# Add and GELU on one core: one load and one store with 64 KB rows in place of two each with 32 KB rows

## Chip, cores, metric

One core of one Trainium2 chip. The metric is device time in microseconds (us) of one execution. Executions of one kernel agree within some 0.3 to 0.5%.

## The reference

```
x, y: float32, 1024 x 4096
z = x + y
out = 0.5 * z * (1 + tanh(sqrt(2/pi) * (z + 0.044715 * z**3)))
```

The kernel uses the same function in the form z * sigmoid(c1 * (z + 0.044715 z^3)). It reads 33.55 MB and writes 16.78 MB.

## The kernel before

Each of the 128 partitions holds 8 rows of x in one piece: TOT = 32768 columns of float32, 128 KB. One tile z keeps all of it, first x, then x + y, then the result. y passes through two buffers of 8192 columns. I call 8192 columns a quarter. The compute engines work in 32 chunks of 1024 columns, while transfers have sizes of their own:

```python
YS = 8192
CH = 1024
PS = 4
loads = [2048, 6144, 8192, 8192, 8192]
stores = [8192, 8192, 8192, 4096, 4096]
...
def load_x(i):
    a, b = lr[i]
    nc.sync.dma_start(out=zt[:, a:b], in_=xv[:, a:b])
def load_y(i):                       # the same into yt[quarter]
    ...
def store(i):
    a, b = sr[i]
    nc.sync.dma_start(out=ov[:, a:b], in_=zt[:, a:b])
...
sp = []
for i in range(len(loads)):
    sp += [(load_x, i), (load_y, i)]
sp += [(store, i) for i in range(len(stores))]
```

All transfers are issued by SP (SyncE), in this order, into one queue. The other engines are POOL (GpSimd), DVE (VectorE) and ACT (ScalarE); PSUM is the second on-chip memory, beside the main one, SBUF. The engines' part per chunk: `add` (POOL; DVE for chunk 0), `sq` (ACT, into PSUM), `stt` (DVE), `sig` (ACT), `mul` (DVE, back into z). DVE runs `mul` of chunk c after `stt` of chunk c+1:

```python
for i in range(-3, C + 1):
    if 0 <= i < C:
        dve.append((stt, i))
        acts.append((sig, i))
    if 0 <= i - 1 < C:
        dve.append((mul, i - 1))
    ...
```

And a y load waits for the adds that free its buffer, a store for the multiplies of its columns.

## Time and profile before

| | before |
|---|---|
| median of 3 executions at the outset | 123.27 us (123.16 to 123.56) |
| span of the profiled execution | 121.5 us |
| busiest compute engine | DVE, 75.5 us (62%) |
| packets of the queue, share of 16 engines' span | 2160, 97.2% |

How to read it: a "span" runs from the first to the last instruction. The 16 DMA engines share a transfer's 128 partition rows, one row to a packet: 8 rows per engine and transfer, then one small packet that signals completion. A share near 100% for the queue means that all 16 engines are moving data nearly all the time. A line of a timeline reads: start in us, duration in us, engine (a q marks its sequencer, which issues transfers), line of the kernel, operation, output<-inputs, count, and in brackets the idle time before it and what ended it. The prediction below shows the lines of before.

### The profile page before, as it was taken

The numbers are of one execution on the slowest core, as the hardware profiler recorded it, in microseconds if no ns is written. First come the engines' busy times: TensorE is split into PE (matmuls) and PEld (weight loads), VectorE is DVE, ScalarE is ACT, GpSimd is POOL, SyncE is SP. The second block draws the span as 40 slices with busy tenths as digits, with TensorE's granted clock in tenths as the row PEclk, the third lists the DMA queues.
The fourth block names the chain that finished last, engine by engine and source line by source line (L and its number), as shares of the span: only waits on it lengthen the run. The fifth ranks groups of instructions, "written<-read, shape, count | busy, mean of one in ns | idle before, by whom it ended". The sixth has DMA issues, their size and how long they took to land.

```text
span 121.5 us, 248 instructions
## 1 busy us (share of the span) xinstructions
DVE 75.5 (62%) x66; ACT 63.8 (52%) x66; POOL 73.0 (60%) x35
## 2 busy tenths in 40 slices
DVE  0035700039999209999996999995999999500000
ACT  4004400068886028788767887883878878100000
POOL 0028000499990099999969999959999990000000
DMA  3999999998989999999999999899999999999993
GB/s 89 421 440 494 413 389 494 391 496 367 496 378 486 389 475 389 475 389 475 389 475 389 475 389 475 345 432 434 424 432 432 442 421 442 421 442 389 426 437 130
DMA packets 2162, 50.35 MB, mean 415 GB/s; under 512 B 240, under 2 KB 240, under 8 KB 240
## 3 DMA queue, kind: packets, MB, share of 16 engines
q1 hardware_dynamic: 2160, 50.33, 97.2%
q14 instruction: 2, 0.02, 0.0%
HBM read 33.55 MB, written 16.78 MB: 414 GB/s over the span
## 4 chain that ended last, share of the span: by engine, by line
DMA 49%; POOL 17%; DVE 16%; SPq 2%; ACT 1%; issue 0%; POOLq 0%
DMA y<-in_y_dram 49%; POOL z L87 17%; DVE z L107 8%; DVE w L98 8%; SPq L70 1%; SPq L77 1%; ACT w L92 1%; POOLq L87 0%
## 5 line engine op out<-in xcount | busy, mean ns | idle before, releaser
L87 POOL TENSOR_TENSOR z<-z,y 128x1024 f32<-128x1024 f32 x31 | 72.8, 2389 | 26.9 <-DMA y<-in_y_dram 26.9
L92 ACT ACTIVATE w<-z 128x1024 f32<-128x1024 f32 x32 | 32.9, 1028 | 38.7 <-POOL z L87 31.4
L98 DVE SCALAR_TENSOR_TENSOR w<-w,z 128x1024 f32<-128x1024 f32 x32 | 39.4, 1232 | 21.1 <-ACT w L92 21.1
L107 DVE TENSOR_TENSOR z<-w,z 128x1024 f32<-128x1024 f32 x32 | 38.8, 1214 | 0.0
L103 ACT ACTIVATE w<-w 128x1024 f32<-128x1024 f32 x32 | 31.4, 981 | 0.4 <-DVE w L98 0.4
L87 DVE TENSOR_TENSOR z<-z,y 128x1024 f32<-128x1024 f32 x1 | 1.2, 1224 | 7.3 <-DMA y<-in_y_dram 7.3
L146 ACT ACT_TABLE_LOAD x1 | 1.3, 1283 | 0.7 <-PEq L172 0.7
L145 DVE MEMSET one<- 128x1 f32 x1 | 0.1, 59 | 0.8 <-PEq L172 0.8
L172 POOL MEMSET const-float32-0.0<- 128x1 f32 x1 | 0.1, 98 | 0.2 <-issue 0.2
L146 ACT ACTIVATE one<-one 128x1 f32<-128x1 f32 x1 | 0.2, 203 | 0.0
L172 POOL MEMSET const-bfloat16-1.0<- 128x1 bf16 x1 | 0.1, 101 | 0.0
L172 POOL MEMSET const-uint8-127<- 128x1 uint8 x1 | 0.1, 101 | 0.0
L172 POOL MEMSET const-float32-1.0<- 128x1 f32 x1 | 0.1, 98 | 0.0
## 6 DMA issues: line engine op xcount, KB each, us to landing
z<-in_x_dram SPq DMA_DIRECT2D x3, 4096.0 KB, 34.2
y<-in_y_dram SPq DMA_DIRECT2D x3, 4096.0 KB, 24.8
out_dram<-z SPq DMA_DIRECT2D x3, 4096.0 KB, 30.3
out_dram<-z SPq DMA_DIRECT2D x2, 2048.0 KB, 17.4
z<-in_x_dram SPq DMA_DIRECT2D x1, 3072.0 KB, 13.8
y<-in_y_dram SPq DMA_DIRECT2D x1, 3072.0 KB, 20.6
z<-in_x_dram SPq DMA_DIRECT2D x1, 1024.0 KB, 4.9
y<-in_y_dram SPq DMA_DIRECT2D x1, 1024.0 KB, 6.9
```

The costliest lines, as they stand in the source:

```text
L70: nc.sync.dma_start(out=zt[:, a:b], in_=xv[:, a:b])
L77: nc.sync.dma_start(out=yt[s][:, o : o + b - a], in_=yv[:, a:b])
L87: eng.tensor_add(out=zt[:, a:b], in0=zt[:, a:b], in1=yt[s][:, o : o + b - a])
L92: nc.scalar.activation(out=wt[c], in_=zt[:, a:b], func=act.Square, scale=root)
L98: nc.vector.scalar_tensor_tensor(out=wt[c], in0=wt[c], scalar=c1, in1=zt[:, a:b], op0=alu.add, op1=alu.mult)
L103: nc.scalar.activation(out=wt[c], in_=wt[c], func=act.Sigmoid)
L107: nc.vector.tensor_mul(out=zt[:, a:b], in0=wt[c], in1=zt[:, a:b])
L145: nc.vector.memset(one, 0.0)
L146: nc.scalar.activation(out=one, in_=one, func=act.Sigmoid)
L172: nc = _bacc.Bacc("TRN2", target_bir_lowering=False, num_devices=1)
```

## The change

The intent is fewer, longer transfers. Two of the five x loads become one, ahead of y of the third quarter, and two of the five stores become one:

```diff
-    loads = [2048, 6144, 8192, 8192, 8192]
-    stores = [8192, 8192, 8192, 4096, 4096]
+    loads_x = [2048, 6144, 8192, 16384]
+    loads_y = [2048, 6144, 8192, 8192, 8192]
+    stores = [16384, 8192, 4096, 4096]
...
-    for i in range(len(loads)):
-        sp += [(load_x, i), (load_y, i)]
+    for i, (a, b) in enumerate(lr):
+        sp += [(load_x, k) for k, r in enumerate(xr) if r[0] == a] + [(load_y, i)]
...
-        add: lambda c: [(f, i) for i in over(lr, *cr[c]) for f in (load_x, load_y)],
+        add: lambda c: [(load_x, i) for i in over(xr, *cr[c])]
+        + [(load_y, i) for i in over(lr, *cr[c])],
```

(Cut: the helper that makes the ranges, and `load_x` reading its own list.)

More of the change, by code (lines that the diff above doesn't have):

```diff
@@ L50, in ranges @@
         return [(e - f, e) for e, f in zip(ends, sizes)]
-    lr, sr, cr = ranges(loads), ranges(stores), ranges([CH] * (TOT // CH))
+    xr, lr, sr = ranges(loads_x), ranges(loads_y), ranges(stores)
+    cr = ranges([CH] * (TOT // CH))
     C = len(cr)
@@ L68, in load_x @@
     def load_x(i):
-        a, b = lr[i]
+        a, b = xr[i]
         nc.sync.dma_start(out=zt[:, a:b], in_=xv[:, a:b])
```

## The prediction

> **What bounds the kernel now.** I read the page first: the engine shares, the DMA slices and the queue line.
>
> ```profile
> DVE 75.5 (62%) x66; ACT 63.8 (52%) x66; POOL 73.0 (60%) x35
> ...
> DMA  3999999998989999999999999899999999999993
> GB/s 89 421 440 494 413 389 494 391 496 367 496 378 486 389 475 389 475 389 475 389 475 389 475 389 475 345 432 434 424 432 432 442 421 442 421 442 389 426 437 130
> DMA packets 2162, 50.35 MB, mean 415 GB/s; under 512 B 240, under 2 KB 240, under 8 KB 240
> ...
> q1 hardware_dynamic: 2160, 50.33, 97.2%
> ```
>
> No compute engine passes 62%, while the packets of the one queue fill 97.2% of 16 engines' span: 0.972 x 121.5 = 118.1 us of DMA time. The DMA digits are 9 nearly everywhere between the first and last slices. The packet count has an exact reading: 15 transfers x (128 rows + 16 small ones) = 2160, so one row of one transfer is one packet, and each engine carries 8 rows and one small packet (the 240 under 512 B, which signal completion) per transfer.
>
> Second, busy shares by stretch, to see whether the queue ever runs dry (columns: stretch, length, busy time of DVE, ACT and POOL, clock, DMA share, GB/s):
>
> ```profile
> 1.70:11.70 10.00, 2.41 (x2) 1.58 (x4) 3.39 (x1) 1.00 1.01 406
> 11.70:60.60 48.90, 31.21 (x28) 27.17 (x28) 32.22 (x14) 1.00 1.00 432
> 60.60:77.60 17.00, 16.06 (x15) 13.60 (x14) 16.06 (x8) 1.00 1.00 432
> 77.60:81.20 3.60, 3.60 (x4) 2.88 (x3) 2.63 (x2) 1.00 1.16 428
> 81.20:120.20 39.00, 22.19 (x20) 17.57 (x19) 18.52 (x8) 1.00 0.97 418
> ```
>
> From 1.7 to 77.6 us the DMA share is 1.00: loads run head to tail. Packets are counted at their start, so 1.16 and 0.97 are neighbours to be read together. The packet records are finer. First packet 1.74 us, last 120.19 us, last completion seen 120.56 us. Transfers end, on their first engine, at 41.23 (y, second quarter), 50.94 (x, third), 60.65 (y, third), 70.36 (x, fourth), 80.62 (y, fourth), then the stores at 90.30, 99.98, 109.66, 114.52 and 119.38. A 4 MB transfer takes 9.7 us, except the last load, 10.26: its last two packets per engine, from 77.6 us on, take 1.3 to 1.8 us instead of 1.21. That loss of about 0.6 us, at the turn from loads to stores, is the only one inside the stream.
>
> Third, the chain of waits, then the last DMA issue in order of time.
>
> ```profile
> DMA 49%; POOL 17%; DVE 16%; SPq 2%; ACT 1%; issue 0%; POOLq 0%
> ```
>
> ```profile
> 104.84 0.33 SPq L81 DMA_DIRECT2D out_dram<-z  x1
> ```
>
> Read alone, the chain suggests that POOL and DVE matter. But it stops at the last multiply; the last store is issued at 104.84 us and waits behind 9.7 us of queued stores. Compute has that much slack at the end. The bound is the byte stream of the DMA queue.
>
> **What the Trainium skill says.** "DMA: Bandwidth & Descriptors", section "Where 436 GB/s comes from", gives a ceiling of 435 GB/s for the 16 ports. The trace agrees: 432 GB/s over 11.70 to 77.60 us. Larger transfers cannot go faster than that; only per-row cost can be saved.
>
> The same page, section "Why small descriptors are slow (HBM only)", speaks of a fixed overhead of about 3 cycles per packet. The packet records fit the kind: median 309, 611, 912 and 1213 ns for rows of 8, 16, 24 and 32 KB. Each 8 KB adds 301 to 302 ns, which leaves about 8 ns fixed per row. A small packet takes 9 ns.
>
> "SBUF — State Buffer", section "The DMA setup-cost knee", puts roughly 2 us on every transfer. Taken as a price per transfer it would promise 4 us here. This trace disagrees with using it so in a queue that is kept full: one transfer's 9 ns signal is followed at once by the next one's first row. The fixed cost shows only where the queue is empty: the first issue starts at 0.74 us and its first packet at 1.74, 1.0 us later.
>
> **The change, part by part.** The order of instructions on DVE, ACT and POOL is unchanged; SP issues two transfers fewer. x of quarters 3 and 4 becomes one transfer ahead of y of quarter 3; the stores of quarters 1 and 2 become one.
>
> Removed: each merge halves 8 rows per engine from two packets to one and drops one small packet: 8 x 8 + 9 = 73 ns. Two merges give 0.15 us. I estimate a 64 KB row at 2 x 1213 - 8 = 2418 ns. Two issues of about 0.4 us on SP go too, but they lie beside a full queue: 0.
>
> Moved: y of quarter 3 now follows all of x, one 4 MB transfer later. It ends where x of quarter 4 ended, less 0.07. The rest is worked from these two rows:
>
> ```profile
> 61.72 18.52 POOL L87 TENSOR_TENSOR z<-z,y 128x1024 f32<-128x1024 f32 x8 [0.94 <-DMA y<-in_y_dram]
> 81.67 18.52 POOL L87 TENSOR_TENSOR z<-z,y 128x1024 f32<-128x1024 f32 x8 [1.43 <-DMA y<-in_y_dram]
> ```
>
> - Adds of quarter 3 start at 61.72 + 9.71 - 0.07 = 71.36 instead of 61.72; POOL idles some 10 us before them.
> - Adds of quarter 4 find their y landed at 81.5, but POOL is busy to 71.36 + 18.52 = 89.88. They start there instead of at 81.67: all later compute is 8.21 us later, bound by POOL (16 adds x 2.315 in one run) rather than by arrivals.
>
> Each store must be issued 1.0 us before the queue reaches it (the delay of the first load):
> - First two quarters: DVE's order puts the multiply of chunk 15 behind chunk 16, so this store waits for quarter 3's first add. Before, the second store was issued 5.84 us after that add's start (67.56); now 71.36 + 5.84 = 77.20, first packet possible at 78.2. The loads end at 80.55. Slack 2.3 us.
> - Quarter 3: issued at 87.9 before (the last semaphore wait on the store line ends there), now 96.1, ready 97.1, due at 109.66 - 9.68 - 0.15 = 99.83. Slack 2.7 us.
> - First half of quarter 4: its last multiply ended near 96.7, now 104.9, ready 105.9, due 109.5. Slack 3.6 us.
> - Last half: 104.84 + 8.21 = 113.05, ready 114.05; due at 114.52 - 0.15 = 114.37 on the first engine and 115.17 on the slowest. Slack 0.3 us on the first engine, 1.1 us on the one that sets the end.
>
> So about 8.2 us of the tail slack goes, and none of it becomes a wait that ends later. Sum: 123.27 - 0.15 = 123.12, with a whisker for the last store: 123.1 us.
>
> **Rivals.** (a) The compute tail becomes the bound. If the queue restarts in 1.5 us rather than 1.0, or POOL runs a few per cent slower without its pause, the last store is late by 0.3 to 1 us: 123.4 to 124.1. For it: the 0.3 us is thin. Against it: the slow engine has 1.1 us. Also, "SBUF — State Buffer", section "Who interferes with whom", says GpSimd and DVE contend when a DVE instruction has two SBUF inputs; after the first chunk DVE always reads one operand from PSUM. The trace agrees: the one POOL add that ran beside DVE's own add took 3.39 us, the 16 above 18.52 / 8 = 2.315 us.
>
> (b) 64 KB rows are moved differently: cut into 32 KB pieces, saving only the two small packets (0.02 us: 123.25), or at a worse rate. A quarter of the bytes loaded plus half of those stored, 16.8 MB, use such rows, or 38.7 us of queue time; each 1% of rate costs 0.4 us. Against a bad rate: the four sizes lie on one straight line.
>
> (c) The slow turn from loads to stores changes. Its 0.6 us may vanish (122.5) or grow with the new store, which joins the queue only 2.3 us ahead: plus 0.5 (123.6). I do not know its cause.
>
> (d) The gain of fewer, larger transfers at some 2 us each: 119 to 120. The gapless queue speaks against it.
>
> **Range and chances.** The main line gives 123.1; executions of before spread from 123.16 to 123.56, so a few tenths are noise. Rivals a and c reach up to about 1 us, mostly upward: 122.6 to 123.9 should hold it 8 times in 10. Faster by 2% means under 120.8, which needs more than the whole idle time of the queue inside the span: 0.01. Slower by 2% means over 125.7, which needs 64 KB rows 6% worse or a late store of 2.5 us: 0.04. Within 2%: 0.95.
>
> **What would show it.** Right: 1872 packets on the queue (2160 - 2 x 144), a 64 KB packet near 2418 ns, POOL's last 16 adds in one run from about 71.4 us, the last store issued near 113.0 us and DMA still at 9 in all late slices. Wrong: 2128 packets (rows cut); 64 KB packets well over 2430 ns; a dip in the DMA slices near 80 us (store of quarters 1 and 2 late) or 114 us (last store late); a queue restart longer than 1.0 us.

## The result

Six executions of each: before 123.19 us median (123.03 to 123.56), after 123.03 us (122.78 to 123.44). The ratio is 0.9988 with a 95% interval of 0.9964 to 1.0012: the same. Ratios here are the mean time of one kernel's fast runs over that of the other's fast runs of the same rounds, so they are not quite the ratio of the medians quoted. The forecast of 123.1 us and "within 2%" held. The parts behind it held less well.

The changed kernel's page and queue lines:

```profile
DVE 75.5 (62%) x66; ACT 63.8 (53%) x66; POOL 73.0 (60%) x35
...
DMA  4999999999999979988899999999987899989992
GB/s 100 414 463 463 414 422 463 411 476 390 476 390 476 530 346 411 606 368 346 379 476 390 476 390 476 390 487 411 611 368 346 390 455 390 476 379 422 422 433 97
...
q1 hardware_dynamic: 1872, 50.33, 97.0%
```

1872 packets is exactly 2160 - 2 x 144, so a 64 KB row is one packet; its record lasts 2418 ns (median). The 7 and 8 in the DMA digits are no idle time by themselves: packets are counted in the slice in which they start, and a 2.4 us packet is nearly a slice long. That is why the next view uses longer stretches (columns as in the prediction: stretch, length, DVE, ACT, POOL, clock, DMA share, GB/s):

```profile
11.70:60.60 48.90, 31.21 (x28) 27.14 (x28) 32.14 (x15) 1.00 1.01 436
60.60:77.60 17.00, 6.47 (x7) 5.33 (x7) 6.45 (x4) 1.00 1.00 432
77.60:81.20 3.60, 3.60 (x4) 2.87 (x4) 3.60 (x3) 1.00 1.23 528
81.20:120.20 39.00, 31.96 (x28) 25.91 (x27) 27.33 (x12) 1.00 0.94 404
```

From 60.6 to 77.6 us POOL worked 6.45 us instead of 16.06, and after 81.2 us 27.33 instead of 18.52: compute has moved towards the end, while the queue kept its 432 GB/s.

The adds of the last two quarters, then SP's issues (early and late; "x2" with one long duration covers two issues and the wait between them):

```profile
71.54 36.99 POOL L89 TENSOR_TENSOR z<-z,y 128x1024 f32<-128x1024 f32 x16 [10.55 <-DMA y<-in_y_dram]
```

```profile
77.36 0.35 SPq L83 DMA_DIRECT2D out_dram<-z  x1
```

```profile
105.08 8.44 SPq L83 DMA_DIRECT2D out_dram<-z  x2
```

One run of 16 adds from 71.54 us, after 10.55 us of idling: as predicted (71.4). First store issued at 77.36 (predicted 77.2), the last at 105.08 + 8.44 - 0.33 = 113.19 (predicted 113.05).

The packet records show what moved in the queue. The interval between the ends of successive transfers, on the engine that ends first (ns):

| interval that ends with | before | after |
|---|---|---|
| x, quarters 3 and 4 | 9706 + 9709 | 19352 |
| y, quarter 4 (the last load) | 10255 | 9718 |
| stores, quarters 1 and 2 | 9681 + 9681 | 19323 |
| store of quarter 3 | 9681 | 9681 |
| last quarter, first half | 4862 | 4863 |
| last quarter, second half | 4863 | 5156 |

So on this engine the merges saved 63 + 39 = 102 ns; the slow turn from loads to stores was gone in this execution (-0.54); and the last store came late on the engines that finish early (+0.29). The end of the execution hangs on the engine that ends last: there the last two intervals are 4863 and 4862 ns before, 4862 and 4862 after, so the late store cost the end nothing. The last packet ended at 119.69 us instead of 120.19.

The gain at the turn was the unexplained part of the prediction (its third rival), so most experiments went there.

### The profile page after: what moved, and what is told of

The parts are those of the page before. It is cut to its first block, busy times and chain, and to the rows that moved or that the text cites. A ratio compares the mean times of both kernels' runs of the same rounds, so it can differ in the third digit from the quotient of the medians.

```text
span 121.1 us, 241 instructions
## 1 busy us (share of the span) xinstructions
DVE 75.5 (62%) x66; ACT 63.8 (53%) x66; POOL 73.0 (60%) x35
## 3 DMA queue, kind: packets, MB, share of 16 engines
q1 hardware_dynamic: 1872, 50.33, 97.0%
## 4 chain that ended last, share of the span: by engine, by line
DMA 46%; DVE 32%; POOL 13%; SPq 1%; ACT 1%; issue 0%; POOLq 0%
DMA y<-in_y_dram 46%; DVE z L109 16%; DVE w L100 16%; POOL z L89 13%; ACT w L94 1%; SPq L72 1%; SPq L79 0%; POOLq L89 0%
```

## The experiments

I measure the loss at the turn as the time by which the last rows of the loads exceed their usual duration (1213 ns for 32 KB), averaged over the 16 engines. It was 0.61 us in the profile of before and 0.02 in that of after.

### 1. Both kernels again, and each half of the change alone

The two kernels unchanged, and the two halves:

```diff
 x_only (from the changed kernel)
-    stores = [16384, 8192, 4096, 4096]
+    stores = [8192, 8192, 8192, 4096, 4096]
 store_only (from the changed kernel)
-    loads_x = [2048, 6144, 8192, 16384]
+    loads_x = [2048, 6144, 8192, 8192, 8192]
```

> The kernel before, unchanged, to see what repeats in its profile. In the profile of before, the last two packets per engine of the loads (from 77.6 us on) ran 1.3 to 1.8 us in place of 1.21, some 0.6 us lost per engine at the turn from loads to stores; in the profile of the changed kernel that loss is nearly absent. Theory A (the loss comes with stores that are queued early, here from 61.2 us on): the slow packets are there again, 0.4 us or more per engine at the turn. Theory B (the loss is chance of one execution): they may be missing here, or show elsewhere. Both: ratio 1.000 within 0.003, span near 121.5 us, 2160 packets on the queue.

> The changed kernel, unchanged. Packet theory (8 rows and one small packet per engine and merge, 73 ns each): 1872 packets, 64 KB packets at 2418 ns median, ratio 0.9988. Theory A (early stores cause the loss at the turn): no slow packets at the turn again, so 0.6 us less there, and ratio nearer 0.995. Theory B: a loss may show up here. Both: the last store is issued near 113.2 us and its first packets start at about 114.05, with gaps of 0.05 to 0.4 us on the engines that finish the store before it early.

> Only the two loads of x merged, the stores as before. Packet theory: one merge, 2016 packets, -0.07 us, ratio 0.9994. Delay theory: the adds of quarter 3 start near 71.5 us and the last store is issued near 113.2 us as in the changed kernel; so this half alone carries the whole shift of the compute. Theory A: the first store is issued near 61.4 us, so the slow packets at the turn are back (0.4 us or more per engine). Theory B: not tied to it. Rival, the merge of x is what removed the loss at the turn: no slow packets.

> Only the first two stores merged, the loads as before. Packet theory: one merge, 2016 packets, -0.07 us, ratio 0.9994. Delay theory: adds of quarter 3 start near 61.7 us, the last store is issued near 104.8 us as before, and no engine has a gap ahead of the last store. Theory A: the first store is issued near 67.5 us, 10 us before the turn, so the slow packets are there. Rival, 64 KB rows of the first store remove the loss at the turn: none.

Five rounds, one chip, before at 123.52 us median (11 runs):

| | median us | ratio to before (95%) | packets | first store issued | loss at the turn |
|---|---|---|---|---|---|
| r_before | 123.48 | 0.9999 (0.9981 to 1.0017) | 2160 | 61.00 | 0.87 us |
| r_after | 123.27 | 0.9975 (0.9954 to 0.9995) | 1872 | 76.85 | 0.78 us |
| x_only | 123.47 | 0.9996 (0.9980 to 1.0013) | 2016 | 61.03 | 0.73 us |
| store_only | 123.57 | 1.0002 (0.9982 to 1.0022) | 2016 | 67.38 | 0.69 us |

The two halves differ where they should: x_only has the late compute, store_only has not.

```profile
71.11 37.00 POOL L89 TENSOR_TENSOR z<-z,y 128x1024 f32<-128x1024 f32 x16 [10.54 <-DMA y<-in_y_dram]
```

```profile
61.56 18.52 POOL L89 TENSOR_TENSOR z<-z,y 128x1024 f32<-128x1024 f32 x8 [0.92 <-DMA y<-in_y_dram]
81.62 18.54 POOL L89 TENSOR_TENSOR z<-z,y 128x1024 f32<-128x1024 f32 x8 [1.54 <-DMA y<-in_y_dram]
```

(x_only, then store_only.) A tenth of a microsecond for the merges cannot be told from noise in these times; only the packet records see it.

The surprise is the loss at the turn. It was in all four, also in the repeat of the changed kernel. So neither merge removes it, and my first theory (the loss comes with stores that are queued early, and a store as late as that of the changed kernel escapes it) missed in the repeat. One number of the repeat stands out:

```profile
76.85 0.35 SPq L83 DMA_DIRECT2D out_dram<-z  x1
```

Here the store was issued half a microsecond earlier than in the first profile of the changed kernel (77.36), with the queue in nearly the same place: the engines started their last two rows of loads at 77.3 and 77.5 us. In the first profile the engines were further apart (0.75 us between first and last end of the first load, 0.44 in the repeat), and a completion counts only when the last engine is done (in before, y of quarter 4 ended on its engines from 80.63 to 81.24 us, and its first add started at 81.67). That gave the second theory: the loss happens only if the store reaches the queue before the last two rows of loads are well under way.

### 2. Hold the first store back

The kernel before, with another order of stores so that the first one waits for chunk 19, and one idle fill on DVE (0.91 us) ahead of that chunk's multiply:

```diff
-    stores = [8192, 8192, 8192, 4096, 4096]
...
+    sr = [(12288, 20480), (0, 8192), (8192, 12288), (20480, 28672), (28672, 32768)]
...
+    def pad(i):
+        nc.vector.memset(idle, 0.0)
...
+        if i - 1 == 19:
+            dve += [(pad, k) for k in range(1)]
         if 0 <= i - 1 < C:
             dve.append((mul, i - 1))
```

(Cut: the lines that use `sr` in place of the list `stores`, and the tile `idle`, 128 x 1024, which nobody reads.)

> The kernel before with its stores in another order, so that the first one waits for a later chunk: columns 12288 to 20480 first (multiply of chunk 19), with one idle fill of 1024 columns on DVE ahead of that multiply (about 1.1 us); the results are the same. It should be issued near 77.9 us and reach the DMA engines near 78.8 us, about 1 us after they start the last but one packet of the loads and 1.2 to 1.8 us before the loads end. Theory A2 (the loss at the turn happens only when the first store is already in the queue when the engines start their last two packets of loads; the profiled run of the changed kernel, with the store issued at 77.36, escaped it, its repeat, with the store at 76.85, did not): excess at the turn under 0.2 us per engine in place of 0.6 to 0.9, no new gap in the queue, ratio about 0.995. Theory B (chance): excess of 0.5 us or more as likely as not, ratio 1.000.

122.80 us median of 5 (122.74 to 122.97), ratio 0.9955 (0.9938 to 0.9973). The loss at the turn is 0.01 us.

```profile
77.75 2.05 SPq L81 DMA_DIRECT2D out_dram<-z  x3
```

```profile
61.61 18.53 POOL L87 TENSOR_TENSOR z<-z,y 128x1024 f32<-128x1024 f32 x8 [0.92 <-DMA y<-in_y_dram]
81.04 18.53 POOL L87 TENSOR_TENSOR z<-z,y 128x1024 f32<-128x1024 f32 x8 [0.90 <-DMA y<-in_y_dram]
```

(Issues of SP, then adds of the last two quarters.) The adds show the turn too, since they start when the last load has landed on the slowest engine: 81.04 - 61.61 = 19.43 us, two transfers of 9.7. In before it was 81.67 - 61.72 = 19.95. In before the first store was issued here:

```profile
61.23 6.66 SPq L81 DMA_DIRECT2D out_dram<-z  x2
```

Nothing was added to the queue and no row changed its size; the later issue, together with the new order of stores, brought 0.5 us. No run here has the new order with an early issue, so this experiment alone does not part the two. after_late in experiment 6 keeps the order of the changed kernel and moves the issue alone at the turn.

### 3. What the later compute costs when the slack is needed

The same edit to both kernels: the last two stores made one, so that it needs the last multiply 4.9 us earlier in the queue.

```diff
 before_big_last
-    stores = [8192, 8192, 8192, 4096, 4096]
+    stores = [8192, 8192, 8192, 8192]
 after_big_last
-    stores = [16384, 8192, 4096, 4096]
+    stores = [16384, 8192, 8192]
```

> The kernel before with its last two stores of 4096 columns made one of 8192: it needs the last multiply of all, 4.9 us sooner in the queue. Slack theory (compute of before has 8.7 us to spare at the last store): the last store is issued near 104.8 us, ready near 105.7, due near 109.7, so no wait; one transfer less, -0.07 us: ratio 0.999, span about 121.4 us. Rival (the end already hangs on compute, as the chain of waits seems to say): several us slower.

> The changed kernel with the same edit. Slack theory: its compute is 8.2 to 8.4 us later, so the last store is issued near 113.2 us, its packets start near 114.05, due at about 109.2 to 110.2; all engines idle for about 4 us and the end comes at 114.1 + 9.7 = 123.8 us of the span, some 3.6 to 4.1 us later than in the changed kernel: 126.7 to 127.4 us, ratio to before 1.027 to 1.033. Rival (the later compute is harmless as such): ratio 0.998.

before_big_last: 123.59 us, ratio 1.0014 (0.9994 to 1.0034), the same. after_big_last: 126.92 us, ratio 1.0285 (1.0265 to 1.0305), as calculated. Around the end of the third quarter's store (before_big_last, then after_big_last):

```profile
108.50:110.50 2.00, 0.00 (x0) 0.00 (x0) 0.00 (x0) 1.00 1.18 508
110.50:113.50 3.00, 0.00 (x0) 0.00 (x0) 0.00 (x0) 1.00 0.88 382
```

```profile
108.50:110.50 2.00, 2.00 (x3) 1.69 (x2) 0.00 (x0) 1.00 0.08 33
110.50:113.50 3.00, 2.33 (x3) 1.01 (x1) 0.00 (x0) 1.00 0.00 0
```

The DMA engines stand still for about 4 us while DVE works through its last chunks. The last store was issued at these times (before_big_last, then after_big_last):

```profile
105.00 0.33 SPq L81 DMA_DIRECT2D out_dram<-z  x1
```

```profile
112.86 0.33 SPq L83 DMA_DIRECT2D out_dram<-z  x1
```

In after_big_last its first packet ran at 113.69 us. The edit that costs nothing before leaves the changed kernel 3.6 us behind before: the merge of x has spent slack that no time of its own shows.

### 4. What a transfer costs in a full queue

The kernel before with 48 transfers of 8 KB rows.

```diff
-    loads = [2048, 6144, 8192, 8192, 8192]
-    stores = [8192, 8192, 8192, 4096, 4096]
+    loads = [2048] * 16
+    stores = [2048] * 16
```

> The kernel before with all loads and stores in transfers of 2048 columns (8 KB rows, 48 transfers of 1 MB). Packet theory: per engine 384 rows in place of 120 at 8 ns each, +2.1 us, and 48 small packets in place of 15 at 9 ns, +0.3 us: +2.4 us, 125.8 us, ratio 1.0195; 8 KB packets at 307 to 309 ns. Rival, about 2 us per transfer: +66 us. Rival, rows of 8 KB and up cost the same per byte: ratio 1.000.

125.24 us, ratio 1.0148 (1.0125 to 1.0170): clear of the noise, though less than the 2% at which the verdict says slower; by 1.8 us and not 2.4.

```profile
q1 hardware_dynamic: 6912, 50.33, 98.1%
```

The intervals between ends of transfers give the true size. In the stores they are 2453, 4863, 9681 and 19323 ns for rows of 8, 16, 32 and 64 KB. Twice one less the next is 43, 45 and 39 ns. So a transfer of eight rows per engine has a fixed part of about 43 ns, not 73: the packet records overlap by a few ns, and I had added their durations. For 33 more transfers that makes 1.4 us. Most loads here ran at 2480 instead of 2453 ns (27 intervals, +0.8), and the loss at the turn is absent (-0.6): together 1.6 us, which is how much later the first engine ends (121.03 us instead of 119.39).

That absence is not what the second theory says: the first store was issued at 65.5 us, 16 us before the loads end.

### 5. Does the loss go with the size of the rows?

```diff
 small_store (from before)
-    stores = [8192, 8192, 8192, 4096, 4096]
+    stores = [2048, 6144, 8192, 8192, 4096, 4096]
 small_load (from before)
-    loads = [2048, 6144, 8192, 8192, 8192]
+    loads = [2048, 6144, 8192, 8192, 6144, 2048]
```

> The kernel before with its first store split, 2048 columns (8 KB rows) and then 6144, both queued long before the turn. One transfer more: +0.07 us. Theory M (at the turn each engine already fetches the first two rows of the store while it still writes its last two rows of loads, and loses time in proportion to those bytes): two 8 KB rows in place of two of 32 KB, excess at the turn about a quarter of 0.7 us, under 0.3 us; ratio 0.997. Rival (the loss is one fixed stall, or depends on the rows of the loads): excess 0.6 us or more, ratio 1.0005.

> The kernel before with its last loads of x and of y split, 6144 and then 2048 columns, so that the last rows ahead of the turn are of 8 KB; stores unchanged and queued early. Two transfers more: +0.15 us. If the loss goes with the rows of the loads that are still being written: excess at the turn under 0.3 us, ratio 0.998. If it goes with the rows of the store alone (two of 32 KB): excess 0.6 us or more, ratio 1.001.

small_store: 123.42 us, ratio 1.0007 (0.9989 to 1.0026), loss 0.57 us. small_load: 123.14 us, ratio 0.9992 (0.9980 to 1.0005), loss 0.37 us, spread over the last 7 or 8 rows of 8 KB, from 78.2 us to the end of the loads. So small rows on one side do not remove the loss, and the idea of two rows fetched ahead, with a loss in proportion to their bytes, fell. It looks more like a stretch of some 2 us before the end of the loads than a number of rows. Why rows_8k has none stays open.

### 6. The changed kernel with both weak spots mended

```diff
 after_late (from the changed kernel)
-    stores = [16384, 8192, 4096, 4096]
+    stores = [16384, 8192, 4096, 2048, 2048]
...
+        if i - 1 == 15:
+            dve.append((pad, 0))
 late_merged (from the kernel of experiment 2)
-    sr = [(12288, 20480), (0, 8192), (8192, 12288), (20480, 28672), (28672, 32768)]
+    sr = [(12288, 20480), (0, 12288), (20480, 28672), (28672, 32768)]
```

(Cut: `pad` of after_late, here a fill of 768 columns.)

> The changed kernel with one idle fill of 768 columns on DVE ahead of the multiply of chunk 15, so that its first store is issued near 77.6 us instead of 76.85 to 77.36, and the last store halved (2048 and 2048 columns, one more transfer, +0.07 us) to take away the late last store. Theory A2: no excess at the turn in any execution, so the two modes of the changed kernel (122.8 to 122.9 and 123.2 to 123.5 us) become the faster one: 122.6 to 122.9 us, ratio 0.9945 to 0.996, range of the runs under 0.3 us; no gap ahead of the last stores. Rival (the modes have another cause): ratio 0.998 and a range of 0.6 us.

> The fastest so far (first store held back past the turn) with its second and third store merged to one of 12288 columns (48 KB rows). One transfer less, -0.07 us against it, which the packet records should show as 2016 packets: 122.7 us, ratio 0.995. No slow packets at the turn. Rival (chance made the held-back version fast): ratio 1.000.

after_late: 122.91 us (122.77 to 123.00), ratio 0.9967 (0.9955 to 0.9978), a little under the gain I expected. late_merged: 122.88 us (122.83 to 122.95), ratio 0.9966 (0.9954 to 0.9977), also short of 0.995. Loss at the turn 0.01 and 0.04 us. The merge in late_merged cannot be seen in the times (late_1 had 0.9955), but the packet records show it: its store of 48 KB rows takes 14500 ns, the two stores of late_1 in its place 9681 + 4862, so 43 ns are saved.

```profile
77.86 0.35 SPq L83 DMA_DIRECT2D out_dram<-z  x1
```

In after_late (the line above) the last two intervals of the queue are 2453 and 2453 ns, so no store was late. Halving the last store can hardly be the gain, since the late store had cost the slowest engine nothing; the later first store is what is left. Its five executions span 0.23 us. The twelve executions of the changed kernel span 122.78 to 123.56; the two that were profiled lie on both sides, 122.89 without the loss and 123.39 with it. That the other ten split for the same reason is an inference.

The loss against the issue of the first store, over all profiles whose last loads have 32 KB rows and whose first store does too or has 64 KB rows:

| first store issued (us) | kernels | loss at the turn (us) |
|---|---|---|
| 61.0 to 67.4 | before, r_before, x_only, store_only, before_big_last | 0.61 to 0.87 |
| 76.85 | r_after | 0.78 |
| 77.03 | after_big_last | 0.20 |
| 77.36 | after | 0.02 |
| 77.75 to 77.86 | late_1, late_merged, after_late | 0.01 to 0.04 |

The last row but one of the loads starts at about 77.3 to 77.7 us on the first engine, the last one 1.2 us later or more, and a store needs some 0.8 us from issue to its first packet. This shows when the loss occurs with these rows, from one profile of each kernel; rows_8k does not fit it. What the engines do in that time is not shown.

## Why the prediction was right, and where not

- **The bound.** Right. The end came with the queue's last packets in every run; late_1 and after_late gained by keeping the queue at its rate, and after_big_last lost because compute left the queue empty. One reading is too strong: the turn is not the only loss inside the stream. The first load's rows also took about 0.5 us per engine more than usual in the profile of before (8 KB rows of up to 1198 ns instead of 309), and 0.65 in that of after.
- **Per-row saving, "Two merges give 0.15 us".** Mechanism right, size off. The merges measured 0.10 us (63 + 39 ns). The term mis-sized was the 8 ns fixed per row plus 9 ns per small packet, which added overlapping records: 43 ns per transfer of eight rows, not 73.
- **64 KB rows.** Right: 1872 packets, 2418 ns.
- **Compute 8.2 us later, with no wait at the end.** Right: in the first profile the first adds, the first store and the last store came within 0.2 us of the forecast, and the last store was issued 8.35 us later than before. The store of quarter 3 came at 95.84 us and not 96.1, because 87.9 us was misread: there the wait for the next store begins, while quarter 3's own store was issued at 87.49 us. "Slack 0.3 us on the first engine" failed in the first profile: the last store's interval grew by 0.29 us there. The forecast rested on a due time that still included the loss at the turn; without it the queue arrived 0.6 us sooner. In the repeat, where the loss was present, the last store's interval was 4863 ns and nothing was late. The "1.1 us on the slowest" held in both: that engine's last interval was 4862 ns each time, so the wait on the early engines did not move the end.
- **The turn (rival c).** Named as open, and it was the largest term in the first pair of profiles. The prediction let it vanish or grow without saying which, and feared a store that joins late; with rows of 32 KB and up, a late enough store is what makes it vanish.

- **The chances.** The reason given for 0.01 is wrong: a queue at 97.2% of 121.5 us is idle for 3.4 us, more than the 2.5 us that "faster by 2%" needs. Nearly all of it lies before the first packet (1.74 us) and after the last (about 1.3 us), where the merges change nothing.

The forecast gain of 0.15 us met a measured 0.16 us between the medians, and that closeness is luck: the merges gave 0.10 us, the noise is larger than either, and the executions of the changed kernel come with and without the 0.5 us of the turn. The time alone does not prove the steps.

## What to carry to other kernels

Where a queue is full from end to end, merging transfers saves only their fixed part, here about 0.04 us each; look instead for the places where the queue slows or empties. A merge that delays what compute needs spends slack that no time shows, until the next edit needs it, so work out each store's issue time against its due time. Where one queue turns from loads to stores, look at the last load packets, and try issuing the first store later, just in time.

## What the Trainium skill lacked or had wrong

- "DMA: Bandwidth & Descriptors" has nothing on a loss where one queue turns from loads to stores. Here it was 0.6 to 0.9 us when a store of 32 KB rows or more was issued 3.4 us or more before the loads end, 0.20 us at 3.0 us (after_big_last), and under 0.05 us at 2.1 to 2.6 us. With 8 KB rows throughout (rows_8k) there was none, though the first store was issued 16 us before the loads end.
- "SBUF — State Buffer", section "The DMA setup-cost knee", prices every transfer at roughly 2 us, mostly as completion latency, and "DMA: Bandwidth & Descriptors", section "Anatomy of one DMA", does so for the path through GpSimd. For a transfer queued behind others in a full queue the runs show 39 to 45 ns (rows of 8 to 64 KB, eight per engine). The pages do not give this second figure.
- No page looked up says outright whether a row of exactly 64 KB stays one packet. It does: 1872 packets, 2418 ns each for the 64 KB rows, at the same rate per byte as smaller ones.
